# Transposes in 64-row tiles and a fixed order in the last steps of a transformer trunk

## The chip, the cores and the metric

The kernel runs on one core of a Trainium2 chip. Its engines work in parallel, each through its own list of instructions in order, and wait for each other through semaphores: TensorE (PE) multiplies and transposes into PSUM, VectorE (DVE) and ScalarE (ACT) read PSUM and write SBUF, GpSimd (POOL) does small elementwise work and issues some DMAs, SyncE (SP) issues most DMAs. The metric is the device time of one execution in microseconds (us); lower is better.

## What is computed

Two sequences, 2048 and 512 rows of 1024 channels, go through an attention layer (banded, 16 heads) and a Fourier layer, and a last RMSNorm. The change lies in the Fourier layer:

```python
h = rmsnorm(x, g)
hg = h.astype(jnp.float32).reshape(b, s, N_FGROUPS, FGROUP_CH)
f = jnp.fft.fftn(hg, axes=(1, 3), norm="ortho").real
gate = h @ w_gate
return x + (f * jax.nn.silu(gate)) @ w_out      # then the final rmsnorm
```

## The kernel before, in words

Every value is kept as a high and a low part, and each product of 128x512 is three matmuls: high by high, high by low, low by high (`matmul3`, L91). To make the two parts of a tile, ACT copies it rounded (the high part) and DVE subtracts the copy (the low part).

The transform over positions is done by residues. 2048 positions are 16 x 128. A **position step** for k1 (`position`, L1363) takes the tiles gr and gs of a radix-16 combination, multiplies them by tables of cosines and sines and gives the rows k1 + 16 k2 and, by symmetry, 16 - k1 + 16 k2, that is two tiles u of 128 rows by 1024 channels. It works in two halves of 512 channels, hf = 0 and 1: the parts of gr and gs (`halves_of`, L1349, tile gp), the sums A and B on PE (tiles Ap and Bp, six matmuls each), then DVE and ACT write u, and at last DVE multiplies u by its gate (L1397). B of both halves lies in one PSUM bank.

Each u is then **turned** (transposed): eight PE transposes of 128x128, four into one PSUM bank (`split_T`, L993, in the earlier steps; `Outs.turn`, L1437, tile tr, in the later ones). The turned tile is split into parts and is the left operand of the output projection.

- The steps for k1 = 0 and 8, 4 and 2 are `step` (L1584). Their projection is `finish` (L1417): for each tile two halves of 24 products (tile fo), added to the residual, then normed (`normed`, L1406: ACT squares and sums, DVE scales the sum, POOL raises it to -1/2, DVE multiplies, SP stores). A step does the positions, finishes the first tile of the step before, turns its own two tiles, finishes the second tile of the step before. DVE at the same time builds the radix sums of the odd residues.
- The steps for k1 = 6, 1, 7, 3 and 5 (in this order; here "step 7" is that of k1 = 7) are pairs of tiles projected together with seven products of 12 matmuls in place of eight (a Strassen form, class `Outs`, L1430). `operands` (L1470) turns the two tiles and makes seven operands out of them: A00, A01 and A11 are quarters of the turned pair, F1 to F4 are sums and differences of quarters, S1 to S4 their parts. `products` (L1483) multiplies: W (A00), Z (S1), W again (S2, accumulated on it after DVE has read it), Z again (S4), X (A01), W again (S3), W again (A11). After each, DVE adds the bank into a residual tile xa or xb. Three hooks put the next step in between: after the first product the parts of the next gr and gs, after the second the next position step (with the S2 product between its halves), after X the next turns and operands. The product of A11 is accumulated on W, so it waits until DVE has read W after S3; the product of S2 waits until DVE has read W after A00.

The order on each engine isn't that of the code: a scheduler takes, at each time of its own model, the first instruction in code order that is ready. An extra edge (`after`, L134, and `seq`, L139, which chains each instruction to the last one of its key) fixes an order where it is written. The Fourier part has few such edges before. Its transposes and position sums take one of five PSUM banks in turn (`bank`, L76, pool psum3, L1258), its projections one of three others (pool psum2).

Of the kernel before, what the change touches and what calls it, by code (L numbers as in the profile page):

```python
# [9 lines left out]
F32 = mybir.dt.float32  # L10
# [9 lines left out]
P = 128  # L20
# [22 lines left out]
def encoder(  # L43
# [32 lines left out]
    def bank(name):  # L76
        return banks[-1].tile([P, 512], F32, tag="bank", name=name)

# [12 lines left out]
    def matmul3(out, a, b, start, stop, more=False):  # L91

        for i, j in ((0, 0), (0, 1), (1, 0)):
            pe(PE.matmul(out, a[i], b[j], start=start and i + j == 0, stop=stop and i == 1, skip_group_check=more))  # L94
# [871 lines left out]
    def fourier_phase(tail):  # L966
        with ExitStack() as es:
# [18 lines left out]
            def split(t, src, lo_engine=DVE):  # L986

                ACT.copy(t[:, 0], src)
                for cs in (slice(0, 256), slice(256, 512)) if lo_engine is POOL else (slice(0, 512),):
                    lo_engine.tensor_tensor(t[:, 1, cs], src[:, cs], f32(t[:, 0, cs]), ALU.subtract)  # L990
                return t[:, 0], t[:, 1]
# [20 lines left out]
            def sumsq(src, name, place=lambda ins: None):  # L1012
                ss = main.tile([P, 8], F32, tag="ss", bufs=2, name=f"ss{name}")
                junk = fp.tile([P, 512], F32, tag="c12", bufs=1, name=f"jk{name}").bitcast(BF16)
                ACT.activation(junk, src, AF.Square, accum_out=ss[:, 0:1])
                return inv_rms(ss, 1, f"inv{name}", place)
# [10 lines left out]
            class Pair:  # L1027
# [37 lines left out]
                def sums(self, i):  # L1065
# [4 lines left out]
                    if i % 2:  # L1070
# [3 lines left out]
                        2: lambda: (F[1], ps[0, 0], ALU.subtract),  # L1074
                        3: lambda: (ps[0, 0], out, ALU.subtract),
                        4: lambda: (ps[0, 1], F[2], ALU.subtract),
# [47 lines left out]
            def prod(out, a, b, ks, first):  # L1124

                for k in ks:
                    cs = slice(k * P, (k + 1) * P)
                    matmul3(out, (a[0][:, cs], a[1][:, cs]), b[k], first and k == 0, k == 3, not first)
# [129 lines left out]
            banks.append(es.enter_context(tc.tile_pool(name="psum3", bufs=5, space=PSUM, reuse_waits="tile")))  # L1258
# [76 lines left out]
            def gated(name, r, place):  # L1335
# [3 lines left out]
                if r[2] is None:  # L1339
                    SP.dma_start(s2, rows(src, (r[0] - off, r[1])))  # L1340
# [8 lines left out]
            def halves_of(name, gr, gs, hf):  # L1349

                out = []
                for i, g in enumerate((gr, gs)):
                    if g is not None:
# [3 lines left out]
                        DVE.tensor_tensor(t[:, 1], gv, f32(t[:, 0]), ALU.subtract)  # L1357
# [3 lines left out]
            last_b = [None]  # L1361

            def position(name, tab, gr, gs, tiles, loads=None, parts=None, between=None, later=None):  # L1363
# [5 lines left out]
                for hf in range(2):  # L1369
# [4 lines left out]
                    def acc(out, tabs, c0, n):  # L1374
                        for i, (w, t) in enumerate(zip(tabs, ts)):
# [4 lines left out]
                            matmul3(out, w, v, i == 0, i == len(ts) - 1)  # L1380

                    a = bank(f"A{name}_{hf}")[:, :260].rearrange("p (g c) -> p g c", g=2)
                    acc(a, (cs, ns), 0, 130)
                    b = bp[:, hf * 256 : hf * 256 + 256].rearrange("p (g c) -> p g c", g=2)
                    acc(b, (sn, cs), P, P)
# [9 lines left out]
                for u, s2 in zip(us, s2s):  # L1395
                    if later is None:
                        DVE.tensor_tensor(u, u, s2, ALU.mult)  # L1397
# [7 lines left out]

            def normed(x2, r):  # L1406

                inv = sumsq(x2, f"f{r[0]}")
                after(DVE.scalar_tensor_tensor(x2, x2, inv[:, 0:1], gfb, ALU.mult, ALU.mult), last_b[0])
                SP.dma_start(out_rows(r), x2)  # L1410
# [6 lines left out]
            def finish(uT, r):  # L1417
                r0 = r[0]
                x2 = residual(r)
                for half in range(2):  # L1420
                    ps = psum2.tile([P, 512], F32, tag="acc", name=f"fo{r0}_{half}")
                    for k in range(KD):
                        matmul3(ps, uT[k], wo[half * KD + k], k == 0, k == KD - 1)
                    xs = x2[:, half * 512 : half * 512 + 512]
                    DVE.tensor_tensor(xs, xs, ps, ALU.add)
                normed(x2, r)

            class Outs:  # L1430
# [6 lines left out]
                def turn(self, i, hf):  # L1437
                    u, r = self.us[i]
                    ps = bank(f"tr{self.n}_{i}{hf}")
                    for k in range(4):  # L1440
                        c0 = (hf * 4 + k) * P
                        PE.transpose(ps[:, k * P : (k + 1) * P], u[:, c0 : c0 + P], ident)
                    v = ps.rearrange("p (k q) -> p k q", k=4)
                    self.ps[i, hf] = v[:, :, ::-1] if r[2] is not None else v

                def own(self, i, hf):
                    t = htile([P, 2, 512], F32R, f"tT{self.n}_{i}{hf}")
                    hi, lo = (t[:, j].rearrange("p (k q) -> p k q", k=4) for j in range(2))
                    ACT.copy(hi, self.ps[i, hf])
# [419 lines left out]
```

## Time and profile before

| | |
|---|---|
| time of three runs | 1580.60, 1583.46, 1583.53 us; median 1583.46 us |
| the profiled execution | 1581.36 us, its span 1579.4 us (about 2.0 us lie around the span) |
| granted TensorE clock | 0.999 |
| instructions | 27487 |
| busy in the span | DVE 1152.7 us, ACT 876.9 us, POOL 446.1 us |
| Fourier position steps | from about 1340 us to the end |
| turns of the steps 0/8, 4, 2 | at 1363.56, 1390.38, 1417.48 us |
| turns of the steps 6, 1, 7, 3, 5 | at 1449.14, 1474.98, 1499.09, 1523.17, 1547.24 us |

A row of the timeline has the start in us from the span's start, the length in us, engine and line, operation, output<-inputs by the program's names, the shape, how many instructions are merged in the row, and in brackets the engine's idle time before it with what ended it. A matmul's length holds its way through the array, so the spacing of starts, not the length, is what one costs in a row of many.

### The profile page before, as it was taken

The numbers are of one execution on the slowest core, as the hardware profiler recorded it, in microseconds if no ns is written. First come the engines' busy times: TensorE is split into PE (matmuls) and PEld (weight loads), VectorE is DVE, ScalarE is ACT, GpSimd is POOL, SyncE is SP. The second block draws the span as 40 slices with busy tenths as digits, with TensorE's granted clock in tenths as the row PEclk, the third lists the DMA queues.
The fourth block names the chain that finished last, engine by engine and source line by source line (L and its number), as shares of the span: only waits on it lengthen the run. The fifth ranks groups of instructions, "written<-read, shape, count | busy, mean of one in ns | idle before, by whom it ended". The sixth has DMA issues, their size and how long they took to land.

```text
span 1579.4 us, 27487 instructions
## 1 busy us (share of the span) xinstructions
PE 1569.1 (99%) x9754; PEld 1321.5 (84%) x9754; DVE 1152.7 (73%) x2793; ACT 876.9 (56%) x2096; POOL 446.1 (28%) x614
## 2 busy tenths in 40 slices
PE   9999999999999999999999999999999999999998
PEld 7888888888888888988888888888888888888886
DVE  6888656877547786378764577669878877989796
ACT  7788535776246784167752476646655554343242
POOL 2575642421404314024222242223112111010110
PEclk9999999999999999999999999999999999999999
DMA  8587695575856567665649556675557569557762
GB/s 302 200 332 283 226 360 210 207 257 202 295 209 222 204 235 272 223 208 220 257 161 334 211 212 227 246 251 204 203 202 259 177 219 407 181 182 299 280 208 80
DMA packets 100996, 373.89 MB, mean 237 GB/s; under 512 B 11267, under 2 KB 22283, under 8 KB 83452
## 3 DMA queue, kind: packets, MB, share of 16 engines
q1 hardware_dynamic: 83148, 298.17, 53.4%
q0 software_dynamic: 16400, 70.04, 11.5%
q10 hardware_dynamic: 1312, 3.94, 0.6%
q8 instruction: 77, 1.26, 0.3%
q14 instruction: 59, 0.48, 0.1%
HBM read 280.84 MB, written 91.26 MB: 236 GB/s over the span
## 4 chain that ended last, share of the span: by engine, by line
PE 95%; DVE 3%; DMA 1%; ACT 1%; issue 1%; POOL 0%; SPq 0%; POOLq 0%; ACTq 0%; DVEq 0%
PE gp L94 14%; PE qp L94 14%; PE spt L94 11%; PE op L94 7%; PE av L590 6%; PE W L94 6%; PE spt L505 6%; PE fo L94 5%; PE vp L94 3%; PE Wo L94 3%; PE Z L94 3%; PE pt L564 3%; PE z L94 2%; PE Zo L94 2%; PE X L94 2%; PE z L1112 1%
## 5 line engine op out<-in xcount | busy, mean ns | idle before, releaser
L94 PE MATMUL gp<-h,wg 128*128 128x512 f32 x960 | 237.8, 396 | 0.0
L94 PE MATMUL qp<-h,wq 128*128 128x512 f32 x960 | 236.9, 395 | 0.0
L524 DVE CUSTOM_DVE_ANT_0 S<-spt,b 128x385 f32<-128x385 f32 (+1 forms) x320 | 156.5, 527 | 105.2 <-PE spt L505 68.0
L94 PEld LDWEIGHTS gp<-h,wg 128*128 128x128 f32 x960 | 174.9, 188 | 37.3 <-issue 1.0
L94 PEld LDWEIGHTS qp<-h,wq 128*128 128x128 f32 x960 | 174.9, 188 | 36.3 <-issue 0.2
L532 ACT ACTIVATE S<-S 128x385 f32<-128x385 f32 (+1 forms) x320 | 188.8, 597 | 19.6 <-DVE S L524 19.3
L572 ACT CAST pts<-pt 128x384 fp32r<-128x384 f32 (+1 forms) x240 | 100.4, 458 | 165.6 <-PE pt L564 156.3
L573 DVE TENSOR_TENSOR pts<-pt,pts 128x384 fp32r<-128x384 f32 (+1 forms) x240 | 114.2, 519 | 23.9 <-ACT pts L572 22.9
L94 PE MATMUL spt<-wo,uT 128*128 128x512 f32 x480 | 120.4, 391 | 0.0
L614 POOL TENSOR_TENSOR uT<-o,uT 128x256 fp32r<-128x256 f32 x75 | 55.5, 740 | 229.6 <-ACT uT L613 224.9
L94 PE MATMUL op<-wo,uT 128*128 128x512 f32 x480 | 118.9, 391 | 0.0
L505 PE MATMUL spt<-kwin,qab 64*128 64x384 f32 (+1 forms) x960 | 118.9, 353 | 0.0
L590 PEld LDWEIGHTS av<-pts,v 128*128 128x128 f32 x576 | 101.4, 188 | 18.8
L94 PE MATMUL fo<-wo,tTu 128*128 128x512 f32 x480 | 115.8, 392 | 0.2 <-ACT wo L1624 0.2
L590 PE MATMUL av<-pts,v 128*128 128x512 f32 (+1 forms) x576 | 115.7, 341 | 0.0
L94 PEld LDWEIGHTS op<-wo,uT 128*128 128x128 f32 x480 | 89.3, 188 | 18.6
L94 PEld LDWEIGHTS spt<-wo,uT 128*128 128x128 f32 x480 | 89.1, 188 | 18.3
L94 PEld LDWEIGHTS fo<-wo,tTu 128*128 128x128 f32 x480 | 88.2, 188 | 17.5 <-ACT wo L1624 0.6
L544 DVE TENSOR_SCALAR S<-S 128x384 f32<-128x384 f32 (+1 forms) x192 | 95.8, 499 | 6.8
L505 PEld LDWEIGHTS spt<-kwin,qab 64*128 64x128 f32 x960 | 74.7, 186 | 28.3 <-issue 26.1
L610 POOL TENSOR_TENSOR o<-o,s 128x256 f32<-128x256 f32 x75 | 55.3, 737 | 134.9 <-DVE o L608 134.5
L564 PEld LDWEIGHTS pt<-ident,S 64*128 64x128 f32 x1328 | 78.4, 138 | 4.2 <-issue 2.1
(333 smaller groups left out, 3195.5 us busy)
## 6 DMA issues: line engine op xcount, KB each, us to landing
wo<-wsd SPq DMA_DIRECT2D x32, 1024.0 KB, 5.2
wq<-wsd SPq DMA_DIRECT2D x31, 1024.0 KB, 7.3
wg<-wsd SPq DMA_DIRECT2D x31, 1024.0 KB, 5.6
x<-x1d SPq DMA_DIRECT2D x40, 512.0 KB, 3.6
b<-b21d SPq DMA_DIRECT2D x40, 512.0 KB, 5.8
b<-rowd SPq DMA_DIRECT2D x40, 384.0 KB, 4.3
xs<-in_x_dram SPq DMA_DIRECT2D x23, 512.0 KB, 6.9
s2d<-gt POOLq DMA_DIRECT2D x40, 256.0 KB, 5.0
```

The source lines that it names most:

```text
L94: pe(PE.matmul(out, a[i], b[j], start=start and i + j == 0, stop=stop and i == 1, skip_group_check=more))
L505: pe(PE.matmul(banks[j][:, 2 + k0 * P : 2 + k1 * P], res["q"][rows, qp, b * P : (b + 1) * P], kwin[g][rows, kp, b * P + k0 * P : b * P + k ...
L524: seq(DVE, DVE.tensor_tensor_reduce(out=s[:, e0:e1], in0=ps[:, 1 + e0 : 1 + e1], in1=st["bias"][:, j, 386 - e1 : 386 - e0][:, ::-1], scale ...
L532: last_exp[0] = seq(ACT, ACT.activation(s[:, e0:e1], s[:, e0:e1], AF.Exp, bias=s[:, 386:387], scale=-1.0, accum_out=s[:, 387:388]))
L544: seq(DVE, DVE.tensor_scalar(s[:, ks], s[:, ks], den, None, ALU.mult))
L564: pe(PE.transpose(ps[h][:, kb, j, :], ss[j][rows, 1 + kb * P : 1 + (kb + 1) * P], ident[rows, rows]))
L572: seq(ACT, ACT.copy(hi, ps[:, k0:k1]))
L573: seq(DVE, DVE.tensor_tensor(lo, ps[:, k0:k1], f32(hi), ALU.subtract))
L590: pe(PE.matmul(to, v, pt, start=n == part == 0, stop=part == 1 and n in (1, len(todo) - 1), skip_group_check=n > 1,))
L610: eng.tensor_tensor(o, o, s, ALU.mult)
L614: low = eng.tensor_tensor(lo, o, f32(hi), ALU.subtract)
L1112: PE.matmul(to, m[part][:, g * P : (g + 1) * P], ch[:, 0, :, odd * P : (odd + 1) * P], start=part == 0, stop=part == 1,)
```

## The change

**Turns in 64-row tiles.** A new `half_turns` replaces `split_T` in `step` and `Outs.turn`: each 128x128 block is transposed as two blocks of 64 rows, one from partitions 0 to 63 and one from 64 to 127, alternating, sixteen for each tile of u, 32 for a step in place of 16. The upper and the lower rows go to different PSUM banks: the first tile of a step to the banks 0 and 1, the second to 2 and 3. So every quarter of a turned tile now lies across two banks, and both quarters of a tile share them. The pool psum3 is closed ahead of step 0/8, and one tile of five banks, the ring, takes its place; the position sums take its banks by count (B the fifth, A the first and the second). The four sample tiles ahead of step 0/8 keep their old turns.

**Order.** In the steps before 6, the turns stand behind the finish of the first pending tile, and the first three matmuls of the next finish behind the turns. In the steps from 6 on, operands, norms and adds stand in one chain on DVE (key "dve") and one on ACT (key "act"); F3 comes ahead of F4; S4, A01, S3 and A11 move to a hook of their own (`others`) behind the first norm; the parts of the second half of gr and gs are chained ahead of the position step; the norm of xb moves into the next step, between the parts of gr and gs. On PE the product of S4 stands behind A of the second half, its last quarter behind B, X behind S4; half of the S3 product (six matmuls) stands ahead of the turns and half behind. Loads of gate rows and stores of results stand behind the loads of the next gr and gs on SP's queue.

```diff
+    def half_turns(tiles):
+        views = []
+        used[0] = 4
+        for i, src in enumerate(tiles):
+            two = ring[0][:, 2 * i : 2 * i + 2]
+            views.append(two.rearrange("p h (k q) -> p k h q", k=KD))
+            for k in range(KD):
+                for h in range(2):
+                    hp = slice(64 * h, 64 * h + 64)
+                    seq("turns", PE.transpose(
+                        two[:, h, 64 * k : 64 * k + 64], src[hp, k * P : (k + 1) * P], ident[hp, hp]
+                    ))
+        return views
...
-                SP.dma_start(s2, rows(src, (r[0] - off, r[1])))
+                after(SP.dma_start(s2, rows(src, (r[0] - off, r[1]))), last_read[0])
...
                     for k in range(KD):
-                        matmul3(ps, uT[k], wo[half * KD + k], k == 0, k == KD - 1)
+                        end = matmul3(
+                            ps, uT[k], wo[half * KD + k], k == 0, k == KD - 1, behind=None if half or k else chain.get("turns")
+                        )
...
                 def operands(self):
-                    self.turn(0, 0)
+                    self.turns()
                     self.own(0, 0)
-                    self.turn(1, 0)
-                    self.turn(1, 1)
-                    self.sums(1)
-                    self.sums(2)
-                    self.turn(0, 1)
+                    for i in (1, 2, 3):
+                        self.sums(i)
+                    self.halve(1)
+                    self.halve(2)
                     self.sums(4)
+
+                def others(self):
+                    self.halve(4)
                     self.own(0, 1)
-                    self.sums(3)
+                    self.halve(3)
                     self.own(1, 1)
...
                     prod(W, A[0, 0], wo[0:4], four, True)
-                    add(xa, 0, W)
+                    seq("dve", add(xa, 0, W))
                     hooks[0]()
                     prod(Z, S[1], ft["T1"], four, True)
-                    add(xb, 1, Z)
+                    seq("dve", add(xb, 1, Z))
...
                     hooks[1](third)
-                    prod(Z, S[4], wo[12:16], four, False)
+                    if last:
+                        end = prod(Z, S[4], wo[12:16], four, False)
+                    else:
+                        prod(Z, S[4], wo[12:16], (0, 1, 2), False, chain["A"])
+                        end = prod(Z, S[4], wo[12:16], (3,), False, chain["B"])
                     add(xa, 1, Z)
                     X = psum2.tile([P, 512], F32, tag="acc", name=f"Xo{self.n}")
-                    prod(X, A[0, 1], wo[4:8], four, True)
-                    add(xa, 0, X)
+                    prod(X, A[0, 1], wo[4:8], four, True, end)
+                    whole = add(xa, 0, X)
+                    for ins in gated_by[-2:]:
+                        after(whole, ins)
+                    chain["turns"] = prod(W, S[3], ft["T3"], (0, 1), False)
                     hooks[2]()
+                    def upper():
+                        prod(W, S[3], ft["T3"], (2, 3), False, chain["turns"])
+                        seq("dve", add(xb, 1, W))
+
                     if not last:
-                        normed(xa, self.us[0][1])
+                        scaled = norm(xa, self.us[0][1], "act", "dve")
+                        upper()
+                        scaled()
+                        hooks[3]()
...
                     if not last:
                         prod(W, A[1, 1], ft["N4"], four, False)
-                        add(xb, 0, W)
-                        normed(xb, self.us[1][1])
-                        return
+                        seq("dve", add(xb, 0, W))
+                        return xb, self.us[1][1]
...
                 if pend:
-                    finish(*pend.pop(0))
-                new = [(split_T(u, f"u{r[0]}", r[2] is not None), r) for u, r in new]
+                    chain["turns"] = finish(*pend.pop(0))
+                new = turned(new)
...
-            finish(*pend.pop(0))
+            chain["turns"] = finish(*pend.pop(0))
             o.operands()
+            o.others()
             finish(*pend.pop(0))
```

152 lines of the change are left out of this document (102 added, 50 removed).

## The prediction

> **What bounds the kernel now.** I read the page first, for the share of each engine and the chain that ended last.
>
> ```profile
> PE 1569.1 (99%) x9754; PEld 1321.5 (84%) x9754; DVE 1152.7 (73%) x2793; ACT 876.9 (56%) x2096; POOL 446.1 (28%) x614
> PE 95%; DVE 3%; DMA 1%; ACT 1%; issue 1%; POOL 0%; SPq 0%; POOLq 0%; ACTq 0%; DVEq 0%
> ```
>
> PE is busy for 99% of the span and carries 95% of the chain, so at first sight each PE cycle saved is time saved. But that is an average. The second view is the busy time by stretch, from one block of turns to the next (columns: stretch, its length, then PE, PEld, DVE, ACT and POOL busy with the number of instructions, the granted clock, DMA share, GB/s).
>
> ```profile
> 1390.38:1417.48 27.10, 26.84 (x137) 22.54 (x136) 26.14 (x36) 12.35 (x22) 2.84 (x3) 1.00 0.45 151
> 1417.48:1449.14 31.66, 31.35 (x158) 26.29 (x157) 29.60 (x41) 8.66 (x18) 1.43 (x2) 1.00 0.63 234
> 1474.98:1499.09 24.11, 24.11 (x125) 20.46 (x125) 21.16 (x37) 10.07 (x21) 4.05 (x4) 1.00 0.70 246
> ```
>
> Here DVE is nearly as full as PE: 26.14 of 27.10 us and 29.60 of 31.66 us where the radix sums are made, 21.16 of 24.11 us in step 7. Whether DVE sets the pace must be read from the order of events. So the third view is PE's timeline from the turns of step 1 (1474.98) to those of step 7 (1499.09), with the turns of step 6 ahead of it.
>
> ```profile
> 1444.34 4.95 PE L94 MATMUL fo<-wo,tTu 128*128 128x512 f32 x21
> 1449.14 1.91 PE L1442 MATMUL tr<-ident,up 128*128 128x128 f32 x16
> 1450.80 6.62 PE L94 MATMUL fo<-wo,tTu 128*128 128x512 f32 x28
> ...
> 1474.98 1.91 PE L1442 MATMUL tr<-ident,up 128*128 128x128 f32 x16
> 1476.65 1.86 PE L94 MATMUL Wo<-fT,S 128*128 128x512 f32 x7
> 1478.35 2.88 PE L94 MATMUL Wo<-wo,tT 128*128 128x512 f32 x12
> 1481.07 0.62 PE L94 MATMUL Zo<-fT,S 128*128 128x512 f32 x2
> 1481.53 2.89 PE L94 MATMUL Wo<-fN,tT 128*128 128x512 f32 x12
> 1484.26 2.43 PE L94 MATMUL Zo<-fT,S 128*128 128x512 f32 x10
> ...
> 1490.83 1.06 PE L94 MATMUL Ap<-gp,tbp 128*128 128x260 f32 x6
> 1491.73 2.03 PE L94 MATMUL Zo<-wo,S 128*128 128x512 f32 x8
> 1493.59 0.86 PE L94 MATMUL Bp<-gp,tbp 128*128 128x256 f32 x6
> 1494.30 1.09 PE L94 MATMUL Zo<-wo,S 128*128 128x512 f32 x4
> 1495.22 2.89 PE L94 MATMUL Xo<-wo,tT 128*128 128x512 f32 x12
> 1497.95 1.30 PE L94 MATMUL Wo<-fT,S 128*128 128x512 f32 x5
> 1499.09 1.91 PE L1442 MATMUL tr<-ident,up 128*128 128x128 f32 x16
> ```
>
> The seams are what the reader is to see. The twelve W products go from 1478.35 to 1481.07, 0.227 us each. Six B products take 0.86 us, but the six A products ahead of them, barely wider, take 1.06 us: about 0.2 us of waiting, inside a row. For whom, DVE's timeline of the same step tells.
>
> ```profile
> 1476.23 0.69 DVE L1450 TENSOR_TENSOR tT<-tr,tT 128x512 fp32r<-128x512 f32 x1 [0.90 <-ACT tT L1449]
> ...
> 1480.64 0.68 DVE L1490 TENSOR_TENSOR x<-x,Wo 128x512 f32<-128x512 f32 x1
> ...
> 1485.07 1.27 DVE L1490 TENSOR_TENSOR x<-x,Wo 128x512 f32<-128x512 f32 x2
> ...
> 1488.23 1.29 DVE L1409 SCALAR_TENSOR_TENSOR x<-x,invf,gfb 128x1024 f32<-128x1024 f32 x1 [0.46 <-POOL invf L88]
> 1489.43 0.68 DVE L1490 TENSOR_TENSOR x<-x,Zo 128x512 f32<-128x512 f32 x1
> 1490.03 1.29 DVE L1357 TENSOR_TENSOR gp<-go,gp 128x512 fp32r<-128x512 f32 x2
> ...
> 1497.62 1.22 DVE L1397 TENSOR_TENSOR up<-up,s2p 128x1024 f32<-128x1024 f32 x1
> ```
>
> After the turns DVE starts at 1476.23 and works through one list, operands, adds, norms, the parts of the next g, with hardly a pause, until the last low part of g ends at 1490.03 + 1.29 = 1491.32. PE's A products, which need it, end and Z goes on at 1491.73. So a step of the last group is a **loop**: turns, 1.25 us to DVE's first subtraction, 15.09 us of DVE's list, 0.41 us for the rest of A, then 7.36 us of PE work (S4, B, X, five of S3) to the next turns. 1.25 + 15.09 + 0.41 + 7.36 = 24.11 us, the period itself. PE is full and DVE's list closes the loop, both at once: the scheduler filled PE just up to what DVE allows. The two adds at 1485.07 hold the second gate: the S2 product may not start ahead of the second of them.
>
> **The change, part by part.** *The turns.* Sixteen transposes go from 1474.98 to 1476.65, 1.67 us, and the seven products behind take 1.70 us where 7 x 0.227 is 1.59: 1.77 us for a block. The attention stage has the new form already, right between products of 128 rows; a block of 24 half transposes, 13 of them in the second row, the other 11 in rows of one that are left out:
>
> ```profile
> 819.43 0.61 PE L94 MATMUL spt<-wo,uT 128*128 128x512 f32 x2
> 819.98 0.65 PE L564 MATMUL pt<-ident,S 64*128 64x64 f32 x13
> ...
> 820.87 0.96 PE L94 MATMUL spt<-wo,uT 128*128 128x512 f32 x3
> ```
>
> The two products end their turn at 819.43 + 2 x 0.227 = 819.88, so going in costs 0.10 us; 24 halves take 0.89 us; the three products behind take 0.96 us where 2 x 0.227 + 0.39 is 0.84, so coming out costs 0.12. That is 1.11 us for 24. Eight more at 0.031 (the 0.89 less some 0.1 at its ends, over 24) give **1.36 us** for 32 and save **0.41 us** a block, 3.3 us in the eight blocks. TensorEngine Tiling (Array Packing) in the Trainium skill, section Key Properties, says that a change of tiling mode drains TensorE; the trace agrees with its 0.10 and 0.12 us, and without a drain the block would cost 1.14 us.
>
> *Where that gain lies on the path.* In steps 0/8, 4, 2 and 6 PE leads, with projections of older tiles to fill its waits: I take the full 4 x 0.41 = 1.64 us, between nothing (DVE at 29.60 of 31.66 us keeps the pace and PE waits longer at A and B) and this. In steps 1, 7, 3, 5 what is saved after the turns lets PE arrive earlier at A, where the low part of g isn't ready. Counted from the first transpose, PE comes 0.41 + 0.10 us earlier by the block and 0.23 by the sixth S3 matmul, which now stands ahead of the turns; more work ahead of A there is none, since S4 is fixed behind A and X behind S4. The gain turns into a wait at A.
>
> *The loop itself.* Its terms in the new order: (a) the first operand needs a whole tile of u, eight pairs of halves in two banks (8 x 0.06 = 0.5 us) and not four transposes of one bank (4 x 0.104 = 0.42): +0.1 us. (b) DVE's list has the same members and the same order but for F3 and F4, which change places: 0. (c) F3's copy on ACT and F1's add on DVE now read the same two banks, and one must wait: between nothing and one copy of about 0.6 us; the F2 add beside it hides nearly all: +0.05. (d) six S3 matmuls ahead of the turns, not five: +0.23. (e) going into the 64-row mode: +0.10. The sum is +0.48 us a loop; bounds 0.1 (the scheduler finds work for some of it) and 1.1.
>
> PSUM — Partial Sum Buffer in the Trainium skill, section on bank collisions, has two engines kept apart on one bank, reads against reads too; by it (c) holds, and without it a loop would cost 0.43. No row before shows such a pair.
>
> *Moved edges.* The norm of xb keeps its place on DVE (1488.23, its wait for POOL with it) and its square on ACT, which is half idle (10.07 of 24.11 us); its store stays behind it on SP. The loads and stores put behind the reads of g on SP already follow them in time. I cost these at nothing; a late gate row would show at L1397, whose last one ends at 1497.62 + 1.22 = 1498.84, 0.25 us ahead of the turns, and 0.75 us in the new order, where the second tile's halves come 0.5 us behind the first's; what is later than that moves the turns. F1 to F4, S1 to S4: same instructions, same shapes, other strides, 0.
>
> *The turns of step 6.* These ran at 1449.14, right behind the last gated row:
>
> ```profile
> 1447.67 1.22 DVE L1397 TENSOR_TENSOR up<-up,s2p 128x1024 f32<-128x1024 f32 x1
> ```
>
> It ends at 1448.89, late because of DVE's radix sums, and PE filled the time with 20 matmuls of the second finish (21 in the row at 1444.34; 28 of its 48 come after the turns). Now that finish's first matmuls stand behind the turns. Its second half, 24 matmuls, has no such edge and can fill 24 x 0.227 = 5.4 us; 20 were needed, and PE arrives 1.2 us earlier, so some 24. I take it as just hidden: 0, at worst 4.5 us and the 1.2 gained.
>
> **Sum**, against the profiled execution of 1581.36 us (span 1579.4): steps 0/8 to 6 give -1.64; the turns of step 1 come 0.33 later by (d) and (e); the loops to 7, 3 and 5 give 3 x 0.48 = +1.44; in the last step the S2 gate again comes by (a) and (c), +0.15. -1.64 + 0.33 + 1.44 + 0.15 = **+0.3 us**. The median of the runs is 1583.46 us, 2.1 us above the profiled one; on it I say **1583.7 us**: no change that can be told. A measurement of this kernel can tell about 0.2%, 3.2 us, so faster is below 1580.3 and slower above 1586.6.
>
> **The rivals.** *PE is the bound in all steps* (faster): the scheduler finds PE work for the wait at A, DVE's list starts early enough, and all blocks count, 8 x 0.41 = 3.3 us, with up to 2 us of small waits at A and B in the steps up to 6 gone by the new order: 1578.2 to 1580.2. For it: PE at 99%. Against: A's 1.06 us, which ends with DVE. Chance 0.20.
>
> *PE stands still ahead of the turns of step 6* (slower): if the scheduler doesn't pull the second half of that finish ahead, the 20 matmuls that hid the wait come after it: 20 x 0.227 = 4.5 us, and the 1.2 us that PE gained before is waited away too, against nothing else gained: 1583.7 + 4.5 + 1.2 = 1589.4. It decides from about 14 matmuls missing there. For it: the row at 1447.67, DVE at 29.60 of 31.66. Against: the edge holds one half only. Chance 0.15.
>
> *The fixed list stalls DVE* (slower): W's add after A11 (the first at 1485.07) now blocks all behind it. The A11 product began at 1481.53, 0.2 us after the add of 1480.64 ended, and ends at 1484.42, 0.65 us ahead of the add that reads it. Each Z matmul that the scheduler puts ahead of it beyond that slack makes DVE, A and the turns 0.23 us later. With all ten ahead that is 2.27 - 0.65 = 1.6 us a step, 6.5 us in four: up to 1590.2; half of that, 1587, is likelier, and it decides from some four matmuls too many. Chance 0.12.
>
> *The halves don't run side by side* and cost as much as whole transposes: 32 x 0.104 = 3.3 us a block, +12.5 us: 1596. The row of 24 in 0.89 us excludes it nearly: 0.01.
>
> **How the numbers follow.** The forecast with its neighbours, 1580.3 to 1586.6, has 0.52. Faster gets 0.20. Slower gets 0.15 + 0.12 + 0.01 = 0.28. The range leaves out the lower half of the faster case and the far end of the slower ones: 1579 to 1589.5 us.
>
> **What would show it.** Right: a block of 32 halves at 1.3 to 1.4 us from the product ahead to the even pace behind; periods of the loops at 24.3 to 24.7 us with an idle stretch of 0.5 to 1.2 us on PE at A, ended by DVE's L1357 line (in the new file another number) or at S2 by the add of W; periods of the earlier steps 0.4 us shorter. Wrong: loop periods near 23.7 us (PE alone is the bound), or a gap of some us ahead of the turns of step 6, or DVE waiting for the A11 product.

## The result, and the profile after

The changed kernel takes 1619.46 us (median of five runs, 1616.61 to 1620.95), the kernel before 1583.40 us beside it (1580.60 to 1583.53). The ratio is 1.0231, with a 95% interval from 1.0216 to 1.0246: 36 us slower. The forecast of 1583.7 us and its range up to 1589.5 us were wrong. The profiled execution took 1620.62 us, its span 1618.9 us, against 1581.36 and 1579.4 us before; the mean granted clock is 0.992 against 0.999. Up to 1300 us the two traces agree within 0.6 us. All that follows lies in the position steps.

First the same two lines of the page as before, of the kernel after: busy time by engine, and the chain that ended last by engine.

```profile
PE 1581.5 (98%) x9882; PEld 1322.6 (82%) x9882; DVE 1153.2 (71%) x2793; ACT 879.4 (54%) x2096; POOL 444.0 (27%) x614
PE 88%; DVE 7%; DMA 2%; issue 1%; ACT 1%; POOL 0%; POOLq 0%; SPq 0%; ACTq 0%; DVEq 0%
```

PE is *more* busy than before by 12.4 us (1581.5 against 1569.1), with turns that should take less time, and its share of the chain has fallen from 95% to 88%. So two things have come in: PE waits, and PE runs slower. The view of PE's waits from 1340 us to the end says for whom (columns: line of the waiting PE instruction, line of the one that ended the wait, us in all, times, longest). Before, it had two rows of 0.3 us each. After:

```profile
PE Wo L120 <- DVE x L1562: 9.1, 6, 2.2
PE ring L97 <- DVE up L1452: 6.6, 2, 5.5
PE ring L97 <- DVE up L1449: 2.2, 1, 2.2
PE ring L120 <- DVE up L1449: 1.9, 3, 1.2
PE ring L120 <- DVE x L1627: 1.8, 1, 1.8
...
PE ring L97 <- DVE invf L113: 1.4, 1, 1.4
...
```

With four rows that are left out (4.2 us) they add up to 27.2 us of waiting. With the 12.4 us of longer PE time that is 39.6 us, and the spans differ by 39.5 us: the loss is in these two sums.

The third view is PE's timeline of one loop, from the turns of step 1 (1492.73) to those of step 7 (1522.98): 30.25 us, where the kernel before took 24.11.

```profile
1492.73 1.21 PE L97 MATMUL ring<-ident,up 64*128 64x64 f32 x32
1493.87 1.65 PE L120 MATMUL Wo<-fT,S 128*128 128x512 f32 x6
...
1508.01 1.12 PE L120 MATMUL ring<-gp,tbp 128*128 128x260 f32 x8
1508.96 1.77 PE L120 MATMUL Wo<-fT,S 128*128 128x512 f32 x7
1512.96 0.75 PE L120 MATMUL Wo<-fT,S 128*128 128x512 f32 x2 [2.23 <-DVE x L1562]
1513.53 2.75 PE L120 MATMUL ring<-gp,tbp 128*128 128x260 f32 x12
1516.08 3.34 PE L120 MATMUL Zo<-wo,S 128*128 128x512 f32 x12
...
1522.98 1.20 PE L97 MATMUL ring<-ident,up 64*128 64x64 f32 x32
```

The block of turns is as cheap as forecast: the next product starts 1.14 us after it. The loss comes later. A and B of the first half end with the row at 1508.01; A of the second half starts at 1513.53 only. In between PE has the last seven matmuls of S2, then 2.23 us of nothing, then two matmuls (1512.96) that are the first of S3: they follow DVE's add of S2's result, the row at 1512.22 below. And behind that the twelve A and B matmuls take 2.55 us, start to start, where they take 1.45 in run e4 below (1461.08 to 1462.53).

What A waits for is seen on DVE, in the same loop:

```profile
1510.03 1.29 DVE L1409 TENSOR_TENSOR gp<-go,gp 128x512 fp32r<-128x512 f32 x2
1511.24 0.41 DVE L1446 TENSOR_TENSOR up<-up,ring 128x254 f32<-128x254 f32 x1
...
1512.22 0.68 DVE L1562 TENSOR_TENSOR x<-x,Wo 128x512 f32<-128x512 f32 x1
1512.82 0.41 DVE L1449 TENSOR_TENSOR up<-up,ring 128x254 f32<-128x254 f32 x1
```

DVE's reads of the first half of B end at 1513.23, and PE writes A of the second half from 1513.53 on. These are different banks, A's second half and B: but they are the same *tile*, the ring. The parts of g, which set the time of A before, were ready at 1511.32 (1510.03 + 1.29): 2.2 us of A's delay go to B's reads, with the add of 0.6 us that stands among them, and the rest is that DVE came late to the parts of g. By this trace alone it could as well be the two matmuls of S3, which end at 1513.41 (1512.96 + 2 x 0.227); that A waits for the reads of B, runs e1 and e10 below show.

The second place is the operands behind the turns. ACT's and DVE's timelines of the same loop (ACT first):

```profile
1493.98 0.59 ACT L1515 CAST tT<-ring 128x512 fp32r<-128x512 f32 x1 [7.53 <-PE ring L97]
1495.32 0.59 ACT L1526 COPY F<-ring 128x512 f32<-128x512 f32 x1 [0.76 <-DVE tT L1516]
1497.38 0.59 ACT L1526 COPY F<-ring 128x512 f32<-128x512 f32 x1 [1.47 <-DVE F L1533]
```

```profile
1494.60 0.69 DVE L1516 TENSOR_TENSOR tT<-ring,tT 128x512 fp32r<-128x512 f32 x1 [2.43 <-ACT tT L1515]
1495.94 1.41 DVE L1533 TENSOR_TENSOR F<-F,ring 128x512 f32<-128x512 f32 x2 [0.65 <-ACT F L1526]
1498.00 0.69 DVE L1533 TENSOR_TENSOR F<-ring,F 128x512 f32<-128x512 f32 x1 [0.66 <-ACT F L1526]
```

ACT's copy at 1495.32 reads the second tile's banks, DVE's subtraction at 1494.60 the first tile's. Both only read. Still ACT waits 0.76 us for DVE, DVE then 0.65 us for ACT, and so on in turns. Before, ACT's two copies of the F operands went in one row, beside DVE:

```profile
1476.10 1.08 ACT L1459 COPY F<-tr 128x512 f32<-128x512 f32 x2
```

In the kernel after, DVE's row of F3 ends 5.96 us behind the start of the turns (1498.00 + 0.69 - 1492.73).

The third place is the turns of step 6 (1459.34): PE stands still for 5.53 us ahead of them, and the 48 finish products behind, which take 11.0 us in run e8 below, take 13.1. The view by stretches has the granted clock (third column from the right) from these turns on:

```profile
1459.34:1461.00 1.66, 1.66 (x31) 1.66 (x32) 0.00 (x0) 0.00 (x0) 0.00 (x0) 0.50 1.06 418
...
1465.00:1467.00 2.00, 2.00 (x9) 1.60 (x8) 1.62 (x3) 1.38 (x3) 0.00 (x0) 0.81 1.03 422
1467.00:1469.00 2.00, 2.00 (x11) 1.64 (x10) 0.87 (x2) 1.10 (x3) 0.00 (x0) 1.00 0.91 330
```

For some 6 us behind the stand-still TensorE runs at half its clock. That, here and in the other places where the clock falls, is the extra busy time.

So the theory was: **the ring is one tile, and its banks are waited for as one**; the edge that holds the finish behind the turns adds a stand-still; the clock adds to both. Its first rival: **the edges**, the new fixed order on PE, DVE and ACT, make the waits whatever the tiles are.

### The profile page after: what moved, and what is told of

It reads as the page before. It is cut to its first block, busy times and chain, and to the rows that moved or that the text cites. A ratio compares the mean times of both kernels' runs of the same rounds, so it can differ in the third digit from the quotient of the medians.

```text
span 1618.9 us, 27743 instructions
## 1 busy us (share of the span) xinstructions
PE 1581.5 (98%) x9882; PEld 1322.6 (82%) x9882; DVE 1153.2 (71%) x2793; ACT 879.4 (54%) x2096; POOL 444.0 (27%) x614
## 4 chain that ended last, share of the span: by engine, by line
PE 88%; DVE 7%; DMA 2%; issue 1%; ACT 1%; POOL 0%; POOLq 0%; SPq 0%; ACTq 0%; DVEq 0%
PE gp L120 14%; PE qp L120 14%; PE spt L120 10%; PE op L120 7%; PE W L120 6%; PE av L618 6%; PE spt L533 6%; PE vp L120 3%; PE Z L120 3%; PE pt L592 3%; PE fo L120 2%; PE z L120 2%; PE X L120 2%; PE ring L120 1%; PE Wo L120 1%
## 5 line engine op out<-in xcount | busy, mean ns | idle before, releaser
L120 PE MATMUL fo<-wo,tTu 128*128 128x512 f32 x480 | 119.3, 402 | 0.0
```

The costliest lines, as they stand in the source:

```text
L120: ins = pe(PE.matmul(out, a[i], b[j], start=start and i + j == 0, stop=stop and i == 1, skip_group_check=more))
```

## The experiments

One table for all runs: the ratio to the kernel before on the same chip with its interval, and the stretches between the starts of the turns in the profiled execution, in us (loops: mean of the three; e2 has its turns in four blocks, counted from the first). In three runs the loops differ much among themselves: 31.00, 25.54 and 25.24 us in e3, 28.85, 31.02 and 33.82 in e7, 28.72, 30.30 and 30.30 in e11.

| kernel | ratio | 0/8 to 4 | 4 to 2 | 2 to 6 | 6 to 1 | loops | last |
|---|---|---|---|---|---|---|---|
| before | 1 | 26.82 | 27.10 | 31.66 | 25.84 | 24.09 | 32.16 |
| after | 1.0231 [1.0216, 1.0246] | 30.69 | 28.19 | 34.14 | 33.39 | 30.29 | 35.30 |
| e1 split tiles | 1.0045 [1.0028, 1.0062] | 26.42 | 26.79 | 31.35 | 32.06 | 24.65 | 32.05 |
| e2 before, one tile | 1.0129 [1.0112, 1.0146] | 24.35 | 29.31 | 33.28 | 27.69 | 29.07 | 33.19 |
| e3 one tile, no edges | 1.0061 [1.0044, 1.0078] | 25.10 | 28.16 | 33.68 | 24.82 | 27.26 | 30.87 |
| e4 split, no edges | 1.0023 [1.0014, 1.0033] | 26.42 | 26.79 | 29.50 | 28.05 | 25.60 | 33.23 |
| e5 split, free finish | 1.0006 [0.9997, 1.0015] | 26.42 | 26.81 | 31.51 | 27.25 | 24.66 | 32.03 |
| e6 one tile, no PE edges | 1.0087 [1.0072, 1.0102] | 25.09 | 28.15 | 33.68 | 25.04 | 27.07 | 34.59 |
| e7 one tile, no DVE/ACT edges | 1.0208 [1.0193, 1.0224] | 30.85 | 28.20 | 34.14 | 31.48 | 31.23 | 33.36 |
| e8 split, filled wait | 1.0062 [1.0046, 1.0077] | 26.41 | 26.81 | 33.78 | 30.52 | 24.65 | 32.01 |
| e9 before, early halves | 0.9995 [0.9986, 1.0004] | 26.42 | 26.81 | 31.40 | 25.83 | 24.10 | 32.16 |
| e10 four banks and one | 1.0154 [1.0138, 1.0170] | 31.12 | 27.00 | 31.52 | 32.80 | 26.81 | 34.19 |
| e11 one tile, free finish | 1.0172 [1.0156, 1.0187] | 25.08 | 28.15 | 33.69 | 26.91 | 29.77 | 35.29 |

**e1: the ring in three tiles, all else as changed.**

```diff
-            return ring[0][:, slot()]
+            n = slot()
+            return ring[2] if n == 4 else ring[n // 2][:, n % 2]
...
-            two = ring[0][:, 2 * i : 2 * i + 2]
+            two = ring[i]
...
-            ring.append(psum4.tile([P, 5, 512], F32, name="ring"))
+            for i in range(2):
+                ring.append(psum4.tile([P, 2, 512], F32, name=f"ring{i}"))
+            ring.append(psum4.tile([P, 512], F32, name="ring2"))
```

> The changed kernel, with its five-bank ring as three PSUM tiles (two pairs of banks and one single bank) in place of one tile of five banks; the banks, the halves, the fixed orders and all edges are kept. Theory 'one tile': the 36 us come from reads and writes of different banks of one tile that are ordered as if they were on the same data. Then ACT's copies and DVE's subtractions of the operands overlap again, A need not wait for the read of B, the loops of the last steps fall from 30.3 to 24.1 to 25 us, and what is left is the wait ahead of the turns of step 6 (some 5 us) with the slow products behind it (some 2 us): 1584 to 1596 us in all. Rival 'edges': the fixed order on PE, DVE and ACT makes the waits. Then the loops stay above 29 us and the time above 1612 us.

Measured: 1588.34 us (1587.57 to 1589.62), loops of 24.65 us. As the theory had it; the rival is out as the cause of the long loops, the same edges being there. ACT's rows of a loop, then DVE's, from the turns at 1504.26 on:

```profile
1505.01 0.59 ACT L1516 CAST tT<-ring 128x512 fp32r<-128x512 f32 x1 [7.77 <-PE ring L98]
1505.51 0.59 ACT L1527 COPY F<-ring 128x512 f32<-128x512 f32 x1
1506.95 0.59 ACT L1527 COPY F<-ring 128x512 f32<-128x512 f32 x1 [0.86 <-DVE F L1534]
```

```profile
1505.63 0.69 DVE L1517 TENSOR_TENSOR tT<-ring,tT 128x512 fp32r<-128x512 f32 x1 [1.11 <-ACT tT L1516]
1506.24 1.40 DVE L1534 TENSOR_TENSOR F<-F,ring 128x512 f32<-128x512 f32 x2
1507.57 0.69 DVE L1534 TENSOR_TENSOR F<-ring,F 128x512 f32<-128x512 f32 x1
```

ACT starts 0.75 us behind the first transpose where it started at 1.25 in the kernel after: it now needs the first tile's sixteen halves alone. Its F1 copy (1505.51) runs beside DVE's subtraction, and DVE goes on without a pause; its row of F3 ends 4.00 us behind the start of the turns, not 5.96. Of these waits one is left, ACT's at 1506.95, and it is for the same pair of banks.

A of the second half no longer waits for B:

```profile
1520.42 1.01 PE L121 MATMUL ring<-gp,tbp 128*128 128x260 f32 x6 [0.27 <-ACT up L1446]
```

It starts ahead of DVE's reads of the first half of B, which go from 1520.63 to 1522.63. The 0.27 us that it does wait end with ACT's read of A's first half, the other bank of the same tile.

**e2: the kernel before, with one tile of five banks from step 0/8 on; nothing else.**

```diff
+            p3.close()
+            psum4 = es.enter_context(tc.tile_pool(name="psum4", bufs=1, space=PSUM, reuse_waits="tile"))
+            ring.append(psum4.tile([P, 5, 512], F32, name="ring"))
...
     def bank(name):
+        if ring:
+            used[0] += 1
+            return ring[0][:, (used[0] - 1) % 5]
```

> The kernel before, with whole turns and no new edge; only the five single-bank tiles of the position steps become one tile of five banks, used in rotation. Theory 'one tile': the loops become longer by at least 3 us each, the whole by at least 15 us: 1598 us or more. Rival 'edges': no change, 1580 to 1586 us.

Measured: 1602.16 us (1601.67 to 1602.71), 20 us above the kernel before; loops of 28.39 to 30.33 us. No half turn and no new edge is in it: this is the price of the one tile alone, in the order of before, which writes and reads the ring four times for a pair of tiles.

**e3 and e4: all new edges off, on one tile and on three.** In both the code order of the change and its halves stay.

```diff
-        after(ins, chain.get(engine))
+        if not isinstance(engine, str):
+            after(ins, chain.get(engine))
         chain[engine] = ins
...
-            after(ins, behind)
...
-                    for ins in gated_by[-2:]:
-                        after(whole, ins)
...
-                    after(SP.dma_start(s2, rows(src, (r[0] - off, r[1]))), last_read[0])
+                    SP.dma_start(s2, rows(src, (r[0] - off, r[1])))
...
-                    after(SP.dma_start(out_rows(r), x2), last_read[0])
+                    SP.dma_start(out_rows(r), x2)
```

> The changed kernel with its one ring tile and its halves, but with all the new fixed orders and edges off (products, turns, operands, norms, loads and stores); the order in which the program is written stays. Theory 'one tile': the time stays most of the way up, 1603 us or more, with loops of 28 us or more. Rival 'edges': the time falls to 1578 to 1588 us.

> Ring as three tiles and all new edges off: what is left of the change are the turns in halves and the order in which the program is written. Both theories: 1576 to 1584 us, the gain of 0.41 us a block on top of the kernel before where PE leads. If it is above 1590 us, neither the tile nor the edges are the cause, and the halves themselves or the written order cost.

Measured: e3 1591.14 us (1589.02 to 1594.63), e4 1585.50 us (1584.44 to 1586.59). Both theories missed e3: the tile alone was to leave it at 1603 or more, the edges alone to bring it to 1588 or less. It is the two together. (Nearly all that e3's loops lose lies in the first of them; the other two are as short as e4's.) In us above the kernel before, from the ratios and 1582 us:

| | all edges | no new edge |
|---|---|---|
| one tile | 36.5 | 9.7 |
| three tiles | 7.1 | 3.6 |

With three tiles the edges cost 3.5 us, with one 26.8. And e4 is 1.5 us above the end of its forecast: with no edges the loops (25.60 us) are longer than with them (24.65). So with three tiles the fixed order of the last steps is worth a microsecond a loop; what the edges cost lies from step 2 to step 1 (63.41 us in e1, 57.55 in e4).

**e5: e1 without the edge of the finish behind the turns.**

```diff
-                            ps, uT[k], wo[half * KD + k], k == 0, k == KD - 1, behind=None if half or k else chain.get("turns")
+                            ps, uT[k], wo[half * KD + k], k == 0, k == KD - 1
```

> The ring as three tiles, all edges kept but one: the first matmuls of a finish no longer stand behind the turns, so the finish can again fill TensorE's wait ahead of the turns of step 6. Theory: what is left of the slowdown with three tiles (1588.3 against 1581.7 us) is that wait; the turns of step 6 stand within 0.5 us of the products ahead of them, the stretch from the turns of step 6 to those of step 1 falls from 32.1 to 26 to 28 us, the whole to 1580.5 to 1584 us. Rival: the loops of 24.65 us against 24.1 are the larger part, and the whole stays at 1586 us or more.

Measured: 1582.82 us (1581.86 to 1584.16), the ratio 1.0006 holds 1. The stretch from 6 to 1 is 27.25 us. With three tiles that one edge was worth 5.5 us by the medians (6.2 by the ratios), 4.8 us in that stretch, and without it the change makes what the forecast said: no difference that can be told. The two rows of e1 at these turns, and the one of e5:

```profile
1447.54 1.79 PE L98 MATMUL ring<-ident,up 64*128 64x64 f32 x32 [4.29 <-ACT jkf L1060]
1449.26 12.12 PE L121 MATMUL fo<-wo,tTu 128*128 128x512 f32 x48
```

```profile
1447.65 1.20 PE L98 MATMUL ring<-ident,up 64*128 64x64 f32 x32
```

In e1 all 48 products of the finish stand behind the turns, the half that has no edge too. In e5 they fill the wait. (The releaser that the row names, ACT, isn't one that the turns need; the gated rows of DVE, which they do need, end within 0.2 us of their start.)

That stretch is still 1.41 us longer than before (27.25 against 25.84). The add of W(A00), before and then in e5, and what follows it there:

```profile
1462.48 0.69 DVE L1490 TENSOR_TENSOR x<-x,Wo 128x512 f32<-128x512 f32 x1 [1.50 <-DMA x<-x1d]
```

```profile
1460.61 0.69 DVE L1563 TENSOR_TENSOR x<-x,Wo 128x512 f32<-128x512 f32 x1 [2.41 <-DMA x<-x1d]
1461.21 0.68 DVE L1410 TENSOR_TENSOR gp<-g1r,gp 128x512 fp32r<-128x512 f32 x1
1461.95 1.83 PE L121 MATMUL ring<-gp,tbp 128*128 128x260 f32 x11 [0.96 <-DVE gp L1410]
```

The add needs the loaded residual tile. Before, DVE made three of the four low parts of g while it waited for that load; the chain "dve" puts the add ahead of them, so A waits too. In e4, with the chain off, DVE makes the same three first, and A starts right behind Z (1461.08) and waits for nothing; no run takes off this chain alone.

**e6 and e7: one tile, with PE's new edges between products off (the turns stay behind the products that are to precede them), or with DVE's, ACT's and the DMAs' off.**

```diff
-            after(ins, behind)
```

for e6, and for e7

```diff
-        after(ins, chain.get(engine))
+        if engine not in ("dve", "act"):
+            after(ins, chain.get(engine))
         chain[engine] = ins
...
-                    for ins in gated_by[-2:]:
-                        after(whole, ins)
```

with the two edges of loads and stores off as in e3.

> The changed kernel with its one ring tile; only TensorE's new edges between products are off (the finish behind the turns, S4 behind A and B, X behind S4, the second half of S3 behind the first). The fixed orders of DVE and ACT and the edges of loads and stores stay. Theory 'one tile costs by what TensorE may do meanwhile': X and S2 go into the waits for the ring, loops fall from 30.3 to 25 to 27 us, the whole to 1590 to 1602 us. Rival 'the fixed lists of DVE and ACT stretch the waits': loops stay above 28.5 us, the whole above 1611 us.

> The mirror of the run before: the one ring tile and TensorE's edges stay; the fixed orders of DVE and ACT and the edges on gated rows, loads and stores are off. Theory 'one tile costs by what TensorE may do meanwhile': loops stay above 28.5 us, the whole above 1611 us. Rival 'the fixed lists': loops of 25 to 27 us, the whole 1590 to 1602 us.

Measured: e6 1595.45 us (1595.03 to 1596.77), e7 1615.59 us (1613.40 to 1620.90). As the theory of TensorE's freedom had it, with loops just above its 25 to 27 us: by the ratios 22.8 us go with PE's edges (0.0144 of 1582 us) and 3.6 with the others, and those only in the median, since the profiled execution of e7 took 1620.90 us. What PE does with its freedom, in a loop of e6 (columns as before):

```profile
1490.59 0.36 PE L120 MATMUL ring<-gp,tbp 128*128 128x260 f32 x1 [0.58 <-ACT gp L1407]
1491.14 0.96 PE L120 MATMUL Xo<-wo,tT 128*128 128x512 f32 x3 [0.19 <-DVE x L1561]
...
1496.05 2.88 PE L120 MATMUL Zo<-wo,S 128*128 128x512 f32 x12
1498.77 1.66 PE L120 MATMUL ring<-gp,tbp 128*128 128x260 f32 x12
```

X, which the change puts behind S4, now goes into the wait of the first half: the row at 1491.14 comes ahead of most of A's and B's matmuls. And S4, which the change puts behind A of the second half, fills the longest wait, ahead of that A (1496.05). The waits are still there (loops of 27.07 us against 24.65 with three tiles), but PE no longer stands idle in the longest of them, and its clock stays up: PE's busy time falls from 1581.5 to 1572.5 us.

**e8: e1 with 18 products that nobody reads, put into the wait ahead of the turns of step 6.**

```diff
             chain["turns"] = finish(*pend.pop(0))
+            for i in range(18):
+                seq("turns", PE.matmul(ring[2], wo[0][0][:, :P], wo[0][0], start=True, stop=True))
             o.operands()
```

> The ring as three tiles with all edges, plus 18 products of 128x512 whose result nobody reads, put into TensorE's wait of 4.3 us ahead of the turns of step 6. Theory 'products right after a stand-still are slow': the 48 finish products behind the turns fall from 11.96 us to 10.9 to 11.3 us although TensorE has more to do, and the whole by about 1 us to 1587 us. Rival 'they are slow for their operands or banks': they stay at 11.9 us, and the whole at 1588 to 1589 us.

Measured: 1591.30 us (1590.84 to 1592.49), against the forecast of a microsecond less. The part on the clock came true, the total did not. The rows:

```profile
1448.01 4.37 PE L1820 MATMUL ring<-wo 128*128 128x512 f32 x18 [2.47 <-DVE up L1450]
1452.32 1.20 PE L98 MATMUL ring<-ident,up 64*128 64x64 f32 x32
1453.45 11.18 PE L121 MATMUL fo<-wo,tTu 128*128 128x512 f32 x48
```

The turns take 1.13 us, start to start, and not 1.72; the 48 products 11.01 and not 11.96: 1.54 us less for the same work, with the granted clock at 1.00 throughout. So it is the clock, low behind the long stand-still, and not operands or banks, that makes what follows slow. But the filling went into the bank that holds B, so it had to wait 2.47 us for DVE's read at L1450, and then held the turns up: the stretch from 2 to 6 is 2.43 us longer than in e1. The rest of the 3 us lies ahead: this kernel's trace is 1.7 us later than e1's from about 20 us on, where the first 48 products of the attention stage have taken 13.3 us and not 12.1, and 2.3 us at the first turns, in work that no edit touches. Two kernels whose first 1300 us hold the same instructions can lie that far apart, which is as much as the smallest effects here.

**e9: the kernel before with the halves in steps 0/8, 4 and 2 alone,** as three tiles; step 6 and the loops as before. The edit takes `half_turns` and `turned` of the change into `step`, without edges.

> The kernel before with the halves in steps 0/8, 4 and 2 alone (two tiles of two banks and one bank); step 6 and the loops keep whole turns in five tiles, and no edge is new. Theory 'the halves save about 0.35 us in each step where TensorE leads': the turns of step 6 come 1.0 to 1.2 us earlier and all behind them too: 1580.5 us, a ratio of 0.9993, not to be told from no change. Rival 'the gain is waited away at step 6': 1581.6 us. If the tiles of two banks cost anything by themselves, it is slower than before.

Measured: 1580.91 us (1579.76 to 1582.89) against 1581.73; the ratio 0.9995 holds 1. The turns are at 1363.88, 1390.30, 1417.11 and 1448.51 us: against before +0.32, -0.08, -0.37 and -0.63, in a trace that is 0.7 us late ahead of the steps. So each step gains 0.3 to 0.4 us, and the loops keep it, but in all it is too little to tell. No version here is shown to beat the kernel before.

**e10: the ring as one tile of the four banks of the turns, and one of the fifth.**

```diff
-            return ring[0][:, slot()]
+            n = slot()
+            return ring[1] if n == 4 else ring[0][:, n]
...
-            ring.append(psum4.tile([P, 5, 512], F32, name="ring"))
+            ring.append(psum4.tile([P, 4, 512], F32, name="ring"))
+            ring.append(psum4.tile([P, 512], F32, name="ringb"))
```

> The changed kernel with all edges; the ring is one tile of the four banks of the turns and one of the bank that holds B. Theory: two waits come from the one tile, the operands' (ACT and DVE read the two pairs in turns, some 1.3 us a loop) and A's second half's (behind DVE's reads of B's first half, the rest of the 5.6 us). The first stays, the second goes: loops of 26 to 27.5 us, the whole 1593 to 1601 us. Rival 'the operands' turns make all of it, by coming late': loops stay above 29 us, above 1610 us. Rival 'B makes all of it': loops of 24.7 us, the whole 1588 to 1590 us.

Measured: 1605.93 us (1605.18 to 1607.66). The loops are as forecast, 26.81 us: taking B out of the ring gives back 3.48 of the 5.64 us a loop, and 2.16 stay with the operands of the two pairs, whose turns on ACT and DVE are the same as in the kernel after:

```profile
1492.68 0.59 ACT L1527 COPY F<-ring 128x512 f32<-128x512 f32 x1 [0.76 <-DVE tT L1517]
1494.74 0.59 ACT L1527 COPY F<-ring 128x512 f32<-128x512 f32 x1 [1.48 <-DVE F L1534]
```

A of the second half now waits 0.37 us for ACT's read of A's first half, no longer for B. The total lies 5 us above the forecast, which had counted loops and step 6 alone. In step 0/8 the banks are taken from the first on, so that both of its B lie among the four banks: there PE stands still 4.17 us ahead of the turns and 1.34 between the two tiles, and the first turns and the stretch behind them come 4.7 us later each than in e1.

**e11: the changed kernel without the finish edge, on one tile** (the diff of e5).

> The changed kernel with its one ring tile and all edges but that of the finish behind the turns. Theory: the stand-still ahead of the turns of step 6 (5.5 us) and the slow products behind it (2.4 us) go, as with three tiles, the loops of 30.3 us stay: 1611 to 1614 us. Rival 'that edge costs more with one tile': below 1608 us.

Measured: 1607.73 us (1606.65 to 1611.07): 11.7 us gone by the medians, 9.3 by the ratios, more than the theory gave, and by the number the rival's. The table shows why: it isn't dearer at step 6 (33.39 to 26.91, 6.5 us), but it acts a second time, at the step from 0/8 to 4 (30.69 to 25.08, 5.6 us), where the kernel after stands still twice ahead of the turns (2.19 and 1.37 us) and runs at half clock behind them. With three tiles there is no wait at that place (26.42 us with the edge and without). A further 1.6 us lies in the first loop, where the clock stayed up (last section).

## Why the prediction was wrong

1. **The step that failed is the loop itself, term (c).** It let F3's copy and F1's add share a pair of banks and took +0.05 us, with 0.6 as the far end; all else that reads or writes the ring was costed at nothing. The unit that is waited for is the tile: all five banks. The ring stood in the diff as one tile, and the forecast never asked what lies in it *together*: A, B and the two pairs. It cost 5.64 us a loop (30.29 against 24.65 in e1), of which 3.48 for B, with some 1.6 of half clock behind its wait, and 2.16 for the operands (e10). PSUM — Partial Sum Buffer in the Trainium skill, section on bank collisions, speaks of two engines on one *bank*; nothing in it asks for different banks to be kept apart, and in e1 different banks are read side by side. So the forecast applied the rule at the wrong size: what waits here are the program's semaphores, which go by the tile.
2. **"Moved edges: I cost these at nothing" failed too, but only with the one tile.** There PE's edges take the fill out of the waits: 22.8 us (e6), 9 to 12 of them the finish edge (e11). With three tiles the whole set costs 3.5 us, the finish edge alone 5.5, so that the others gain.
3. **The turns of step 6: the rival came true.** Its price was 5.7 us; with three tiles it is 5.5 (e1 against e5). What failed is "its second half has no edge and can fill": none of its 24 matmuls was put ahead of the turns in e1 or after. Why the scheduler left them is not settled; only the first half has the edge, and it stands first in the code.
4. **The clock was in no term.** PE's busy time is 13.3 us longer than in e5 (1581.5 against 1568.2), which has the same PE instructions. That is a third of the loss.
5. **Right: the block of turns.** Forecast 1.36 us; in e1 1502.80 + 6 x 0.227 to 1504.26 is 0.10 in, 1.13 for the 32 halves, and the six products behind take 1.50 for 1.36: 1.37 us in all.
6. **Right: the gain in steps 0/8 to 6**, once the tiles are split: -0.40, -0.31 and -0.31 us in e1's first three stretches, for the 0.41 that was said. The third of them ends at DVE's gated rows and not at PE's work, so it says less than the other two. On one tile the gain is buried.
7. **Right, once the tiles are split: the loop,** +0.56 us (24.65 against 24.09) for +0.48, and along the path that was laid out: in e1, from 1504.26 on, 1.37 us to DVE's first subtraction, 15.09 of DVE's list, 0.55 for the rest of A and 7.64 of PE work, where the kernel before has 1.25, 15.09, 0.41 and 7.36. The 0.14 more at A was in no term. The sum, +0.3, is 1.2 us in e5, and that doesn't mean that each term held: the stretch from the turns of step 6 to those of step 1 was to change by -0.08 (-0.41 + 0.33) and is 1.41 us longer.
8. The rival "the fixed list stalls DVE" got 0 to 4 us of the loss (e7); a stall of its kind, at another add than the one it named, is what e5 has left from step 6 to step 1. "PE is the bound" is out: with three tiles the loops are longer than before, 24.65 us for 24.09, and not shorter.

So the mechanisms that were priced were mostly priced well, and the one that decided was not in the list. The chances had 0.28 for slower and nothing beyond 1596 us.

## What to carry to other kernels

When a change replaces several buffers by views of one, list every reader and writer of the new buffer and suppose that each waits for each, until the trace shows otherwise; here that list, four operands of ACT and DVE and the two halves of A and B, cost 29 us (1.0231 against 1.0045), some nine times the 3.3 us that the transposes were to gain. An edge that fixes an order is cheap as long as nothing waits, and dear where a wait needs filling: price edges and waits together, never one by one. And a wait of TensorE of two microseconds or more can cost twice, once for itself and once for the half clock behind it: some 1.6 us here.

## What the runs showed of the hardware

The granted clock can fall to 0.50 when TensorE stands still for a few microseconds, and the fall can come after work has begun again. In the kernel after, waits of 1.12, 1.20 and 1.83 us left it at 1.00; the wait of 2.23 us in the first loop did this (view by stretches, clock third from the right):

```profile
1512.96:1514.00 1.04, 1.04 (x5) 0.95 (x6) 0.27 (x1) 0.00 (x0) 0.00 (x0) 0.78 0.84 126
1514.00:1515.00 1.00, 1.00 (x6) 1.00 (x6) 0.00 (x0) 0.00 (x0) 0.00 (x0) 0.50 0.88 360
...
1516.00:1517.00 1.00, 1.00 (x5) 0.81 (x4) 0.20 (x1) 0.44 (x2) 0.42 (x1) 0.52 0.00 0
```

The row from 1512.96 and the one from 1516.00 place the low stretch: from about 0.6 us after PE is back at work (44% of 1.04 us at half clock) to 1516.96, 3.4 us; the next row, from 1517.00, is at 1.00. For a wait of 2.23 us that costs 1.6 us more: 2.55 for 1.45 in A and B, 3.18 for 2.72 in S4. In the other two loops the fall comes 1.0 and 1.5 us after PE is back and lasts 3.4 us again. Behind the 5.53 us of step 6 the clock is low from the start of the turns, for 6.4 us.

The length of the wait does not decide alone. In the first loop of e11 a wait of 2.22 us at the same place left the clock at 1.00:

```profile
1500.53 0.73 PE L120 MATMUL Wo<-fT,S 128*128 128x512 f32 x2 [2.22 <-DVE x L1562]
1501.10 1.61 PE L120 MATMUL ring<-gp,tbp 128*128 128x260 f32 x12
1502.54 2.91 PE L120 MATMUL Zo<-wo,S 128*128 128x512 f32 x12
```

A and B take 1.44 us there, and the loop 28.72 us where the other two of e11, with the same wait and the fall, take 30.30: the half clock alone is 1.6 us. Waits of 2.16 us in e3, 2.45 in e11 and 2.47 in e8 left the clock up as well, while waits of 1.96 in e3 and 2.02 in e7 brought it down. What decides between them, no run here settles.

TensorE: Matmul & The Clock Gate in the Trainium skill, section on the clock gate, says that the clock halves after an idle window of about 3.4 us that runs freely; the halving and the length of the low stretch agree, but here less than 3.4 us of idle time was enough. That equal waits end differently would fit a window that runs freely.
